# A decoder layer on one core: the front's planning constants, and the last tile's output in four pieces

## The chip, the cores and the metric

The kernel runs on one core of a Trainium2 chip. The metric is the device time of one execution in microseconds (us), as a median over runs. The core's engines are TensorE (PE in the profile, with its weight loads as PEld), VectorE (DVE), ScalarE (ACT), GpSimd (POOL) and SyncE (SP), which here only issues transfers. Each engine works through its own list of instructions in order, and engines wait for each other through semaphores.

## The reference

One post-norm decoder layer on x of 512 tokens by 1024 columns, all in float32:

```python
h = x @ w_in                                   # q, k, v, u, z: 512 columns each
attn = moba_attention(rope(q), rope(k), v)     # 8 heads of 64, block-sparse, causal
sg = gelu(u) * (W_s @ layer_norm(gelu(z)) + b) # gMLP gating in chunks of 128 tokens
mix = concat(rms_norm(attn), rms_norm(sg)) @ w_out
x = layer_norm(alpha * x + mix)
ffn = (silu(x @ w_gate) * (x @ w_up)) @ w_down # hidden width 2816
out = layer_norm(alpha * x + ffn)
```

## The kernel before

**Products.** Every float32 product is made of three matmuls of split operands: high times high, high times low, low times high. `mm3` issues such a triple (lines 252 to 254 of the profile). `split` makes the two halves: the high half is a copy on ACT (line 239) or, where `near` is set, on DVE (line 237); the low half is a subtraction on DVE or POOL (line 240). `split_dram` makes the low half in another way: ACT writes the negated high half (line 247), and a transfer issued by POOL adds the weights from DRAM onto it (line 248).

**Order.** The program is written as operations with a cost, a rank and dependences, given to `Order.op`. `Order.plan` runs a list schedule over five engines with these costs: the engine that is free first takes, of the operations that are ready, the one of lowest rank, and the result is the order in which the instructions are put on their engines. A cost thus changes no work; it changes the planned moment at which things are ready, and by that the order. `MM` is the planned cost of a triple of 512 columns. `RANK` gives the rank of each kind of work, and `TABLE` the cost of an ACT table change.

**Stages.** The front (about 0 to 225 us) has the v projection, then the parts of `SEQ`: q and k projections with rotary (`q0` to `q3`), attention of two heads each (`a0` to `a3`), the z and u projections, and `s` (`spatial`, `gmlp_norm`). `UNITS` is the order of the four query tiles in a head; a unit is scores, maximum, exponent, normalisation (line 464), transposes (line 471) through one PSUM bank, and the split of the transposed probabilities. `gmlp_norm` goes through four token tiles: a square on ACT (line 584), the power -0.5 on POOL (line 282), a scaling on DVE (line 586), four transposes (line 591), and a split. Then `out_half(4)` multiplies the gated half by the lower half of w_out, and `out_half(0)` the attention half by the upper half, whose operand `at_split` makes (lines 663 and 665). Projections and out-projections have rank `fill`: PE does them when nothing else is ready.

**First norm.** `layer_norm` runs tile by tile after `out_half(0)`: `add`, statistics (line 693), their sum (694), `rsqrt_col` (lines 281 and 282), then the normalised halves. With how = "A" or "P", ACT scales (line 706), DVE multiplies by the gain (708), and the bias is added at line 717: on DVE with "A", on POOL with "P". With "D" DVE does both steps in two fused operations per half (lines 702 and 713). Then each half is transposed (766) and split.

**FFN.** From there to about 440 us eleven `Pair`s of gate and up blocks are multiplied by a scheme with fewer block products (line 850). The first four pairs (`EARLY`) have their first blocks split ahead, in the front. `EARLY_LO` gives for each of their eight blocks how the low half is made: "M" is `split_dram`, "D" is `split` with DVE. Then the down projection runs to 557 us, and `finish` normalises and stores each tile: add (line 1012), `layer_norm` as `LN2` says ("ADAD"), and one store of 128 x 512 per half on SP (line 1017).

Groups of weights are named: `W(..., group="o1")` is w_out's second row tile. A group in `WHI` has its high half on DVE, one in `WPOOL` its low half on POOL. The groups that are passed are q0 to q3, z, u and o0 to o7; blocks of gate and up go through `whole`, which asks `EARLY_LO` and neither list.

Of the kernel before, what the change touches and what calls it, by code (L numbers as in the profile page):

```python
# [9 lines left out]
ALU = mybir.AluOpType  # L10
AX = mybir.AxisListType.X

P = 128
# [3 lines left out]
NT = S // P  # L17
# [12 lines left out]

SAME, CROSS, DMA_LAT, MM, MM256 = 0.15, 0.19, 1.9, 0.681, 0.36
GROW, GROW_LAT = 0.9, 10
SEQ = ('q1', 'a1', 'q0', 'z', 'q2', 'a0', 'u', 'q3', 's', 'a2', 'a3')
RANK = {"w": 5.0, "rope": 10.0, "att": 4.0, "gelu": -8.0, "z": -2.0, "s": -13.5, "fill": 15.0, "sq": -6.0, "ln": -10.5, "ffn": 8.0, "evac": 3.0}


UNITS = (2, 0, 3, 1)
NORM = "AADA"  # L40
LN1, LN2, LNT = "APAA", "ADAD", 0.3
WHI = ('o0', 'o2', 'q1')
WPOOL = ('e0', 'e1', 'e3', 'o1', 'o2', 'o4', 'z')
ROPE, ZSUB, ZMUL, ZG, ZB = "P", "P", "P", "P", "P"


class Buf:
# [139 lines left out]
def build(tc, cp, wp, ap, ps, xt, xtok, w_vqk, w_zu, w_out, w_gu, w_dn, wsp, cst, rows, cols, out):  # L187
    nc = tc.nc
    od = Order()
    V, A, PL, PE = nc.vector, nc.scalar, nc.gpsimd, nc.tensor  # L190
# [5 lines left out]
    def dve(n, fn, r, w, per=1.042, **k):  # L196
        od.op("DVE", 0.066 + 0.001 * per * n, fn, r, w, **k)
# [4 lines left out]
    def dma(kb, fn, r, w, **k):  # L202
        od.op("SP", max(0.46, kb / 352.0), fn, r, w, **k)

    def pe(n, fn, r, w, **k):
        od.op("PE", n, fn, r, w, **k)

    def const(shape, tag=None, dtype=F32):
        return od.buf(cp, shape, dtype, tag)

    def work(shape, tag, bufs=1, dtype=F32):
        return od.buf(ap, shape, dtype, tag, bufs)
# [4 lines left out]
    def prob(dtype=F32):  # L217
        return work([P, S], "pr", 4, dtype)

    def small(n):  # L220
        return work([P, n], "sm", 24)

    def bank(tag, bufs):
        return od.buf(ps, [P, S], F32, tag, bufs)

    def pj():
        return bank("pj", 4)
# [22 lines left out]
    def mm3(cost, o, lh, ll, rh, rl, start, stop, r, w, **k):  # L250
        def fn():
            PE.matmul(o(), lhsT=lh(), rhs=rh(), start=start, stop=False)  # L252
            PE.matmul(o(), lhsT=lh(), rhs=rl(), start=False, stop=False)  # L253
            PE.matmul(o(), lhsT=ll(), rhs=rh(), start=False, stop=stop)  # L254

        pe(cost, fn, r, w, **k)

    class W:


        def __init__(self, src, tag=None, mid=None, group=None):
# [10 lines left out]
            every = slice(0, WCH)  # L272
            dma(512, lambda: nc.sync.dma_start(raw.t, src), [], [raw], base=RANK["w"])
            if mid is not None:
                mid(raw)
            split(WCH, lambda: raw.t, lambda: self.hi(every), lambda: self.lo(every), [raw], hk, lk, group in WPOOL,
                  near=group in WHI, base=RANK["w"])

# [10 lines left out]
    mhalf, ones = const([P, 32]), const([P, 2])  # L289
# [3 lines left out]
    def row(i):  # L293
        b = work([P, D], "kl", 2)
        dma(512, lambda: nc.sync.dma_start(b.t, bass.AP(tensor=rows.tensor, offset=rows.offset + 3 * S + i * D,
                                                        ap=[[0, P], [1, D]])), [], [b], base=RANK["rope"])
        return b
# [16 lines left out]
    def v_step(c, kk, raw, wh, wl):  # L314
        k = 2 * c + kk
        cs = slice(kk * 512, kk * 512 + 512)
        xr = prob()
        dma(256, lambda: nc.sync.dma_start(raw.t[:, cs], w_vqk[c][:, cs]), [], [(raw, kk)], base=RANK["w"])
        split(512, lambda: raw.t[:, cs], lambda: wh.t[:, cs], lambda: wl.t[:, cs],
              [(raw, kk)], [(wh, kk)], [(wl, kk)], base=RANK["w"])  # L320
        pieces = ((0, 1), (1, NT)) if k == 0 else ((0, NT),)
        for t0, t1 in pieces:
            def piece(t0=t0, t1=t1, ts=slice(t0 * P, t1 * P)):
                sub = [(k, t) for t in range(t0, t1)]
                dma(64 * (t1 - t0), lambda: nc.sync.dma_start(xr.t[:, ts], xt[k][:, ts]), [], [(xr, t0)], base=RANK["w"])
                split((t1 - t0) * P, lambda: xr.t[:, ts], lambda: xh.t[:, k, ts], lambda: xl.t[:, k, ts], [(xr, t0)],
# [295 lines left out]
    xk = work([P, NT, D], "xl")  # L622
# [3 lines left out]
    def out_half(c0, spare, left, done, wide=None):  # L626
        ws = [W(w_out[c0 + k], spare if k == 3 else None, group=f"o{c0 + k}") for k in range(4)]
        for t in range(NT):
            ts = slice(t * P, t * P + P)
            b = [bank("sc", 2), bank("sc", 2)] if t == wide else [pj(), pj()]  # L630
            for k in range(4):
                for hf in range(2):
                    def one(k=k, hf=hf, t=t, ts=ts, b=b, hs=slice(hf * 512, hf * 512 + 512)):
                        lh, ll, keys = left(k, t, ts)
                        mm3(MM, lambda: b[hf].t, lh, ll, lambda: ws[k].hi(hs), lambda: ws[k].lo(hs), k == 0, k == 3,
                            [*keys, *ws[k].key], [b[hf]])

                    one()
            done(t, b)
# [42 lines left out]

    HV = [slice(0, 512), slice(512, 1024)]

    def layer_norm(t, add, done, how):

        keys = [(xk, (t, 0)), (xk, (t, 1))]
        y = lambda i: xk.t[:, t, HV[i]]
        st, mv, rs, nmr = small(12), small(2), small(1), small(1)
        g, b = LN  # L690
        for i in range(2):
            add(i, keys[i])
            dve(512, lambda i=i: V.bn_stats(out=st.t[:, 6 * i:6 * i + 6], in_=y(i)), [keys[i]], [(st, i)])
        dve(12, lambda: V.bn_aggr(out=mv.t, in_=st.t.rearrange("p (a b) -> p a b", b=6)), [st], [mv])
        rsqrt_col(rs, lambda: mv.t[:, 1:2], [mv], 1, 1.0, LN_EPS)
        if how != "D":
            dve(1, lambda: V.scalar_tensor_tensor(out=nmr.t, in0=mv.t[:, 0:1], scalar=-1.0, in1=rs.t, op0=ALU.mult,
                                                  op1=ALU.mult), [mv, rs], [nmr])
        for i in range(2):
            k, gi, bi = [keys[i]], lambda i=i: g.t[:, HV[i]], lambda i=i: b.t[:, HV[i]]  # L700
            if how == "D":
                dve(560, lambda i=i, gi=gi: V.scalar_tensor_tensor(
                    out=y(i), in0=y(i), scalar=mv.t[:, 0:1], in1=gi(), op0=ALU.subtract, op1=ALU.mult), [mv, g, *k], k,
                    lock=True)
            else:
                act(512, lambda i=i: A.activation(y(i), y(i), AF.Identity, bias=nmr.t, scale=rs.t), [rs, nmr, *k], k,
                    aps=2)
                dve(512, lambda i=i, gi=gi: V.tensor_tensor(out=y(i), in0=y(i), in1=gi(), op=ALU.mult), [g, *k], k,
                    lock=True)
        for i in range(2):  # L710
            k, bi = [keys[i]], lambda i=i: b.t[:, HV[i]]
            if how == "D":
                dve(560, lambda i=i, bi=bi: V.scalar_tensor_tensor(
                    out=y(i), in0=y(i), scalar=rs.t, in1=bi(), op0=ALU.mult, op1=ALU.add), [rs, b, *k], k,
                    lock=True)
            else:
                either("P" if how == "P" else "D", 512, lambda E, i=i, bi=bi: E.tensor_tensor(
                    out=y(i), in0=y(i), in1=bi(), op=ALU.add), [b, *k], k)
            done(i, k)
# [197 lines left out]
            self.gated(c, self.h1, self.i1, 0, -1.0)  # L917

    pairs = [Pair(p) for p in range(NP)]
    EARLY, EARLY_LO = 4, "MMMMMMMM"  # L920
    EARLY_SLOTS = (("wr", "wr"), (0, 1), ("wr", "wr"), (0, 1))
    for p in range(EARLY):
        blks = [whole(Raw(p, 3 * i, EARLY_SLOTS[p][i]), 2 * p + i) for i in range(2)]
# [47 lines left out]
    yb = [[pj(), pj()], [pj(), pj()], [bank("sc", 2), bank("sc", 2)], [bank("tp", 1), bank("pv", 1)]]  # L971

    last = work([P, KT, S], "xh", 1, F32R)
# [16 lines left out]
    def down_mm(f, t, hf, w):  # L990
        w, (hh, hl), keys = w
        ts = slice(t * P, t * P + P)
        hs = slice(hf * 512, hf * 512 + 512)
        mm3(MM, lambda: yb[t][hf].t, lambda: hh()[:, ts], lambda: hl()[:, ts],
            lambda: w.hi(hs), lambda: w.lo(hs), f == 0, f == FT - 1, [*w.key, *keys], [yb[t][hf]])

    TAIL = 6
    for f in range(FT - TAIL):
        w = down_w(f)
# [6 lines left out]
    def finish(t):  # L1006
        for i in range(2):
            for f in wt:
                down_mm(f, t, i, wt[f])

        def add(i, key):
            dve(512, lambda: V.scalar_tensor_tensor(out=xk.t[:, t, HV[i]], in0=xk.t[:, t, HV[i]], scalar=ALPHA,
                                                    in1=yb[t][i].t, op0=ALU.mult, op1=ALU.add),
                [yb[t][i], key], [key])

        def done(i, key):
            dma(256, lambda: nc.sync.dma_start(out[t * P:t * P + P, HV[i]], xk.t[:, t, HV[i]]), key, [])

        od.base = RANK["ffn"] - 0.1 * (t + 1)
        layer_norm(t, add, done, LN2[t])  # L1020
        od.base = RANK["ffn"]

    for t in range(NT):
        finish(t)
# [65 lines left out]
```

## Time and profile before

| | us |
|---|---|
| median of 3 runs | 566.88 (566.67 to 567.62) |
| the profiled execution | 566.79 |
| its span in the trace | 565.0 |
| PE busy in the span | 545.7 |

The profiled execution is 1.79 us longer than its span, which is what lies around the traced instructions, and 0.09 us under the median. A busy PE is not a PE at its peak: the ends of matmuls are modelled. The granted clock of TensorE is a share of full speed: 1.00 is 2.4 GHz and 0.50 is 1.2 GHz. Idle time of PE is 565.0 - 545.7 = 19.3 us, and some of it is before the first and after the last matmul.

### The profile page before, as it was taken

How to read it: one execution, taken by the hardware profiler on the slowest of the kernel's cores; microseconds unless marked ns; L12 is line 12 of the kernel's file. 1: busy time of each engine (PE TensorE's matmuls, PEld its weight loads, DVE VectorE, ACT ScalarE, POOL GpSimd, SP SyncE). 2: the span in 40 equal slices, each digit the busy share in tenths (PEclk: the TensorE clock that was granted, in tenths of full speed). 3: DMA queues.
4: the chain of work that ended last, by engine and by line, in shares of the span. 5: the costliest groups of instructions: out<-in, count | busy, mean ns of one | idle time of the engine just before them, and what ended most of it. 6: DMA issues, size and time to landing. Idle time of an engine off the chain costs nothing.

```text
span 565.0 us, 8788 instructions
## 1 busy us (share of the span) xinstructions
PE 545.7 (97%) x3360; PEld 488.1 (86%) x3360; DVE 406.6 (72%) x701; ACT 290.0 (51%) x492; POOL 158.2 (28%) x120
## 2 busy tenths in 40 slices
PE   9999999999699999999999999999999999999994
PEld 6887888888488878999999999999999888888883
DVE  5645868889885879979998788878877623324485
ACT  6324787687774768745444544554455432323211
POOL 0016229823311531234452342333322200000011
PEclk9999999999699999999999999999999999999998
DMA  8746412144811898635432333233124333232311
GB/s 261 261 133 160 129 59 93 57 143 134 307 43 45 244 280 205 171 109 187 131 131 89 137 98 106 97 113 113 37 75 150 117 107 105 82 113 79 108 74 74
DMA packets 23241, 72.85 MB, mean 129 GB/s; under 512 B 3104, under 2 KB 3616, under 8 KB 23200
## 3 DMA queue, kind: packets, MB, share of 16 engines
q1 hardware_dynamic: 22048, 68.11, 37.2%
q0 software_dynamic: 1152, 4.19, 4.0%
q8 instruction: 26, 0.43, 0.3%
q14 instruction: 15, 0.12, 0.1%
HBM read 66.00 MB, written 2.10 MB: 121 GB/s over the span
## 4 chain that ended last, share of the span: by engine, by line
PE 84%; DMA 5%; ACT 5%; DVE 3%; issue 2%; SPq 1%; POOL 0%; DVEq 0%; POOLq 0%; ACTq 0%
PE pj L850 19%; PE sc L850 16%; PE pj L252 11%; PE pj L253 11%; PE pj L254 11%; DMA wr<-w_gu 2%; PE sc L252 2%; PE sc L253 2%; PE sc L254 2%; PE pv L488 2%; PE tp L471 1%; DMA wr<-w_out 1%; DMA zg<-w_gu 1%; DMA qk<-qk 1%; PE pv L252 1%
## 5 line engine op out<-in xcount | busy, mean ns | idle before, releaser
L240 DVE TENSOR_TENSOR wl<-wr,wh 128x1024 fp32r<-128x1024 f32 (+1 forms) x56 | 71.7, 1284 | 63.0 <-ACT wh L239 62.9
L239 ACT ACTIVATE wh<-wr 128x1024 fp32r<-128x1024 f32 (+1 forms) x59 | 58.9, 999 | 82.4 <-PE sc L254 54.0
L850 PE MATMUL pj<-qk,wh 128*128 128x256 f32 x352 | 64.4, 283 | 0.0
L850 PE MATMUL sc<-xh,wh 128*128 128x256 f32 x352 | 64.3, 283 | 0.0
L850 PEld LDWEIGHTS pj<-qk,wh 128*128 128x128 f32 x352 | 55.0, 192 | 0.0
L850 PEld LDWEIGHTS sc<-xh,wh 128*128 128x128 f32 x352 | 54.9, 192 | 0.0
L282 POOL TENSOR_TENSOR sm<-sm,only 128x1 f32<-128x1 f32 (+2 forms) x17 | 18.7, 1099 | 124.8 <-DVE sm L281 124.8
L850 PE MATMUL pj<-V,wh 128*128 128x256 f32 x288 | 52.6, 283 | 0.0
L850 PE MATMUL pj<-qk,wl 128*128 128x256 f32 x176 | 50.0, 284 | 0.1
L850 PE MATMUL sc<-xh,wl 128*128 128x256 f32 x176 | 49.9, 283 | 0.0
L252 PE MATMUL pj<-wh,xh 128*128 128x512 f32 x114 | 47.0, 412 | 0.0
L253 PE MATMUL pj<-wl,xh 128*128 128x512 f32 x114 | 45.0, 395 | 0.0
L850 PEld LDWEIGHTS pj<-V,wh 128*128 128x128 f32 x288 | 45.0, 192 | 0.0
L850 PE MATMUL pj<-V,wl 128*128 128x256 f32 x144 | 40.8, 283 | 0.0
L254 PE MATMUL pj<-wh,xl 128*128 128x512 f32 x96 | 37.9, 395 | 0.0
L240 POOL TENSOR_TENSOR wl<-wr,wh 128x1024 fp32r<-128x1024 f32 x7 | 17.7, 2523 | 69.5 <-ACT wh L239 66.6
L239 ACT ACTIVATE wh<-tp 128x512 fp32r<-128x512 f32 x33 | 19.6, 595 | 30.1 <-PE sc L850 20.4
L850 PEld LDWEIGHTS pj<-qk,wl 128*128 128x128 f32 x176 | 33.8, 192 | 0.3 <-DVE wl L240 0.3
L850 PEld LDWEIGHTS sc<-xh,wl 128*128 128x128 f32 x176 | 33.8, 192 | 0.0
L850 PE MATMUL sc<-ug,wh 128*128 128x256 f32 x176 | 32.2, 284 | 0.9 <-ACT wh L239 0.9
L850 PEld LDWEIGHTS sc<-ug,wh 128*128 128x128 f32 x176 | 27.5, 192 | 1.2 <-ACT wh L239 1.1
L253 PE MATMUL pj<-wl,pr 128*128 128x512 f32 x72 | 28.0, 390 | 0.0
(338 smaller groups left out, 1510.6 us busy)
## 6 DMA issues: line engine op xcount, KB each, us to landing
wr<-w_dn SPq DMA_DIRECT2D x22, 512.0 KB, 3.3
wr<-w_gu SPq DMA_DIRECT2D x20, 512.0 KB, 3.4
zg<-w_gu SPq DMA_DIRECT2D x18, 512.0 KB, 3.4
kl<-w_gu SPq DMA_DIRECT2D x14, 512.0 KB, 3.3
wr<-w_vqk SPq DMA_DIRECT2D x8, 512.0 KB, 3.6
wr<-w_zu SPq DMA_DIRECT2D x8, 512.0 KB, 3.5
wr<-w_out SPq DMA_DIRECT2D x8, 512.0 KB, 4.2
wr<-w_vqk SPq DMA_DIRECT2D x8, 256.0 KB, 4.5
```

The lines of the kernel that those rows point to most:

```text
L239: act(n, lambda: A.activation(hi(), src(), AF.Copy), rs, ws_hi, **k)
L240: either("P" if far else "D", n, lambda E: E.tensor_tensor(out=lo(), in0=src(), in1=hi().bitcast(F32), op=ALU.subtract), [*rs, *ws_hi], ws_lo,
L252: PE.matmul(o(), lhsT=lh(), rhs=rh(), start=start, stop=False)
L253: PE.matmul(o(), lhsT=lh(), rhs=rl(), start=False, stop=False)
L254: PE.matmul(o(), lhsT=ll(), rhs=rh(), start=False, stop=stop)
L282: od.op("POOL", 0.3 + 0.165 * n, lambda: PL.tensor_tensor(out=o.t, in0=v.t, in1=mhalf.t[:, :n], op=ALU.pow), [v, mhalf], [o], lock=True)
L471: PE.transpose(tp.t[:, j * P:j * P + P], p.t[:, j * P:j * P + P], ident.t)
L488: PE.matmul(pv.t[:, j * P:], lhsT=vs.t[:, j, h, :], rhs=pt.t[:, j * S:j * S + w], start=j == 0 and i == 0, stop=j == NT - 1 and i == 1)
L850: PE.matmul(o, lhsT=lh(w), rhs=buf.t[:, s + rh, x], start=first and side == k == i == 0, stop=k == 3 and i == 2, skip_group_check=True)
```

## The change

The planned cost of a triple is 0.643 instead of 0.681 in the v, q, k, z and u projections; the out and down projections keep 0.681 under the name `MMD`. Three ranks and the step between the first norm's tiles have other numbers. The first norm's bias goes to POOL for tiles 0 and 2 instead of tile 1. The high halves of o1 and o3 are made on DVE. Of the eight early blocks, the first and the last have their low half made by DVE. The last tile's bias step is made in four pieces of 256 columns, each stored at once, by ACT's and SP's queues in turn; and a power operation on constants, whose result nobody reads, is put on POOL ahead of the last tile's own.

```diff
--- before.py
+++ after.py
@@ -30,18 +30,20 @@
 
 
 
-SAME, CROSS, DMA_LAT, MM, MM256 = 0.15, 0.19, 1.9, 0.681, 0.36
+SAME, CROSS, DMA_LAT, MM, MMD, MM256 = 0.15, 0.19, 1.9, 0.643, 0.681, 0.36
 GROW, GROW_LAT = 0.9, 10
 SEQ = ('q1', 'a1', 'q0', 'z', 'q2', 'a0', 'u', 'q3', 's', 'a2', 'a3')
-RANK = {"w": 5.0, "rope": 10.0, "att": 4.0, "gelu": -8.0, "z": -2.0, "s": -13.5, "fill": 15.0, "sq": -6.0, "ln": -10.5, "ffn": 8.0, "evac": 3.0}
+RANK = {"w": 5.0, "rope": 10.0, "att": 4.0, "gelu": -8.0, "z": -2.0, "s": -13.5, "fill": 15.0, "sq": -6.0, "ln": -5.8, "ffn": 10.8, "evac": 4.6}
 
 
 UNITS = (2, 0, 3, 1)
 NORM = "AADA"
-LN1, LN2, LNT = "APAA", "ADAD", 0.3
-WHI = ('o0', 'o2', 'q1')
-WPOOL = ('e0', 'e1', 'e3', 'o1', 'o2', 'o4', 'z')
+LN1, LN2, LNT = "PAPA", "ADAD", 0.05
+WHI = ('o0', 'o1', 'o2', 'o3', 'q1')
+WPOOL = ('o1', 'o2', 'o4', 'z')
 ROPE, ZSUB, ZMUL, ZG, ZB = "P", "P", "P", "P", "P"
+
+EARLY, EARLY_LO = 4, "DMMMMMMD"
 
 
 class Buf:
@@ -632,7 +634,7 @@
                 for hf in range(2):
                     def one(k=k, hf=hf, t=t, ts=ts, b=b, hs=slice(hf * 512, hf * 512 + 512)):
                         lh, ll, keys = left(k, t, ts)
-                        mm3(MM, lambda: b[hf].t, lh, ll, lambda: ws[k].hi(hs), lambda: ws[k].lo(hs), k == 0, k == 3,
+                        mm3(MMD, lambda: b[hf].t, lh, ll, lambda: ws[k].hi(hs), lambda: ws[k].lo(hs), k == 0, k == 3,
                             [*keys, *ws[k].key], [b[hf]])
 
                     one()
@@ -682,7 +684,7 @@
 
     HV = [slice(0, 512), slice(512, 1024)]
 
-    def layer_norm(t, add, done, how):
+    def layer_norm(t, add, done, how, last=None):
 
         keys = [(xk, (t, 0)), (xk, (t, 1))]
         y = lambda i: xk.t[:, t, HV[i]]
@@ -690,6 +692,10 @@
         g, b = LN
         for i in range(2):
             add(i, keys[i])
+            if last and i == 1:
+                v = small(1)
+                od.op("POOL", 0.5, lambda: PL.tensor_tensor(out=v.t, in0=ones.t[:, 0:1], in1=mhalf.t[:, 0:1], op=ALU.pow),
+                      [ones, mhalf, keys[1]], [v], lock=True)
             dve(512, lambda i=i: V.bn_stats(out=st.t[:, 6 * i:6 * i + 6], in_=y(i)), [keys[i]], [(st, i)])
         dve(12, lambda: V.bn_aggr(out=mv.t, in_=st.t.rearrange("p (a b) -> p a b", b=6)), [st], [mv])
         rsqrt_col(rs, lambda: mv.t[:, 1:2], [mv], 1, 1.0, LN_EPS)
@@ -709,6 +715,14 @@
                     lock=True)
         for i in range(2):
             k, bi = [keys[i]], lambda i=i: b.t[:, HV[i]]
+            if last:
+                for j in range(2):
+                    c = slice(512 * i + 256 * j, 512 * i + 256 * j + 256)
+                    dve(280, lambda c=c: V.scalar_tensor_tensor(
+                        out=xk.t[:, t, c], in0=xk.t[:, t, c], scalar=rs.t, in1=b.t[:, c], op0=ALU.mult, op1=ALU.add),
+                        [rs, b, *k], [(xk, (t, i, j))], lock=True)
+                    last(j, c, (xk, (t, i, j)))
+                continue
             if how == "D":
                 dve(560, lambda i=i, bi=bi: V.scalar_tensor_tensor(
                     out=y(i), in0=y(i), scalar=rs.t, in1=bi(), op0=ALU.mult, op1=ALU.add), [rs, b, *k], k,
@@ -917,7 +931,6 @@
             self.gated(c, self.h1, self.i1, 0, -1.0)
 
     pairs = [Pair(p) for p in range(NP)]
-    EARLY, EARLY_LO = 4, "MMMMMMMM"
     EARLY_SLOTS = (("wr", "wr"), (0, 1), ("wr", "wr"), (0, 1))
     for p in range(EARLY):
         blks = [whole(Raw(p, 3 * i, EARLY_SLOTS[p][i]), 2 * p + i) for i in range(2)]
@@ -991,7 +1004,7 @@
         w, (hh, hl), keys = w
         ts = slice(t * P, t * P + P)
         hs = slice(hf * 512, hf * 512 + 512)
-        mm3(MM, lambda: yb[t][hf].t, lambda: hh()[:, ts], lambda: hl()[:, ts],
+        mm3(MMD, lambda: yb[t][hf].t, lambda: hh()[:, ts], lambda: hl()[:, ts],
             lambda: w.hi(hs), lambda: w.lo(hs), f == 0, f == FT - 1, [*w.key, *keys], [yb[t][hf]])
 
     TAIL = 6
@@ -1017,7 +1030,13 @@
             dma(256, lambda: nc.sync.dma_start(out[t * P:t * P + P, HV[i]], xk.t[:, t, HV[i]]), key, [])
 
         od.base = RANK["ffn"] - 0.1 * (t + 1)
-        layer_norm(t, add, done, LN2[t])
+        def piece(j, c, key):
+            if j:
+                dma(128, lambda: nc.sync.dma_start(out[t * P:t * P + P, c], xk.t[:, t, c]), [key], [])
+            else:
+                od.op("ACT", 0.1, lambda: A.dma_start(out[t * P:t * P + P, c], xk.t[:, t, c]), [key], [])
+
+        layer_norm(t, add, done, LN2[t], piece if t == NT - 1 else None)
         od.base = RANK["ffn"]
 
     for t in range(NT):
```

## Rows read from the trace of the kernel before

**Rows 1.** The page's list of busy time (share of the span) and instructions.

```profile
PE 545.7 (97%) x3360; PEld 488.1 (86%) x3360; DVE 406.6 (72%) x701; ACT 290.0 (51%) x492; POOL 158.2 (28%) x120
```

**Rows 2.** Windows of 5 us: busy PE, PEld, DVE, ACT, POOL, clock, DMA share, GB/s.

```profile
140.00:145.00 5.00, 1.60 (x11) 1.17 (x9) 4.54 (x10) 4.49 (x10) 2.28 (x2) 0.85 0.76 207
145.00:150.00 5.00, 3.00 (x11) 2.36 (x11) 3.78 (x7) 4.48 (x9) 2.37 (x2) 0.50 0.98 366
150.00:155.00 5.00, 5.00 (x20) 3.88 (x19) 3.98 (x11) 2.26 (x5) 1.38 (x2) 0.62 0.90 309
```

**Rows 3.** What PE waited for: us in total, times, longest.

```profile
PE pj L591 <- DVE ug L586: 2.7, 1, 2.7
PE tp L471 <- DVE sm L281: 2.0, 1, 2.0
...
PE sc L432 <- DMA qk<-qk: 1.1, 1, 1.1
```

**Rows 4.** Timeline around PE's longest stall (start us, us, engine, line, operation).

```profile
139.97 1.32 ACT L663 ACTIVATE xh<-atr,only 128x512 fp32r<-128x512 f32 x2
...
143.22 0.73 DVE L665 SCALAR_TENSOR_TENSOR xh<-atr,only,xh 128x512 fp32r<-128x512 f32 x1
144.41 1.23 DVE L240 TENSOR_TENSOR wl<-wr,wh 128x1024 fp32r<-128x1024 f32 x1 [0.46 <-ACT wh L239]
145.56 0.74 DVE L586 SCALAR_TENSOR_TENSOR ug<-ug,sm,only 128x512 f32<-128x512 f32 x1
```

**Rows 5.** The chain that ended last, after the stall and near the end (start, us, what).

```profile
150.19 0.43 PE pj L254
...
548.98 0.23 PE tp L252
```

**Rows 6.** One window of 20 us in the first norm, columns as in rows 2.

```profile
205.00:225.00 20.00, 17.37 (x128) 15.77 (x127) 15.82 (x31) 16.83 (x25) 4.99 (x6) 1.00 0.95 227
```

**Rows 7.** Timeline in the first norm: POOL's bias addition, and PE's waits.

```profile
206.05 1.30 POOL L717 TENSOR_TENSOR xl<-xl,kl 128x512 f32<-128x512 f32 x1 [1.69 <-DVE xl L708]
...
209.51 0.39 PE L850 MATMUL pj<-V,pth 128*128 128x256 f32 x1 [0.92 <-ACT V L239]
...
215.07 0.63 PE L766 MATMUL tp<-only,xl 128*128 128x128 f32 x4 [0.74 <-issue]
```

**Rows 8.** Single lines of code: duration of one, ns, min/median/max, first and last start.

```profile
L247 ACT ACTIVATE wl<-wr x2: 1044/1045/1046, 207.4 to 213.5; 128x1024 fp32r<-128x1024 f32 x2
L237 DVE TENSOR_SCALAR wh<-wr x4: 686/694/695, 23.1 to 185.5; 128x1024 fp32r<-128x1024 f32 x4
L717 DVE TENSOR_TENSOR xl<-xl,kl x10: 643/684/687, 199.7 to 555.6; 128x512 f32<-128x512 f32 x10
L240 DVE TENSOR_TENSOR wl<-kl,wh x12: 1207/1225/2817, 258.5 to 427.1; 128x1024 fp32r<-128x1024 f32 x12
L566 DVE SCALAR_TENSOR_TENSOR ug<-pj,only,ug x8: 476/480/486, 127.6 to 134.0; 128x256 f32<-128x256 f32 x8
```

**Rows 9.** Timeline of the last tile's norm on DVE.

```profile
557.17 0.69 DVE L1012 SCALAR_TENSOR_TENSOR xl<-xl,pv 128x512 f32<-128x512 f32 x1 [0.92 <-PE pv L254]
...
558.94 1.40 DVE L702 SCALAR_TENSOR_TENSOR xl<-xl,sm,kl 128x512 f32<-128x512 f32 x2
560.26 1.41 DVE L713 SCALAR_TENSOR_TENSOR xl<-xl,sm,kl 128x512 f32<-128x512 f32 x2
```

**Rows 10.** POOL's powers in the second norm, first and last of four.

```profile
538.75 0.56 POOL L282 TENSOR_TENSOR sm<-sm,only 128x1 f32<-128x1 f32 x1 [96.85 <-DVE sm L281]
...
559.10 0.99 POOL L282 TENSOR_TENSOR sm<-sm,only 128x1 f32<-128x1 f32 x1 [7.61 <-DVE sm L281]
```

**Rows 11.** The last store's issue on SP, and issues to landing (KB each, median us).

```profile
561.69 0.33 SPq L1017 DMA_DIRECT2D out<-xl  x1
...
rt<-rt SPq DMA_DIRECT2D x32, 64.0 KB, 2.0
...
out<-xl SPq DMA_DIRECT2D x8, 256.0 KB, 2.1
```

## The prediction

> **What bounds the kernel now.** I read the page's busy times first: PE is busy 545.7 of 565.0 us [rows 1], so the kernel is bound by TensorE, and 19.3 us are all that any order can win. The change adds and removes no matmul. The questions are where those 19.3 us lie, and which of them an order of issue can reach.
>
> The last tile's addition starts on DVE at 557.17, after a wait for the last matmul [rows 9], so 565.0 - 557.1 = 7.9 us are the tail. Next I went through the span in windows. Only one stretch has PE clearly idle: between 140 and 150 us PE is busy 1.60 and 3.00 us of 5 [rows 2], which leaves 3.4 + 2.0 = 5.4 us. The list of PE's waits names the same place: 2.7 us for line 586 and 2.0 us before a transpose, while the front before it has one wait of 1.1 us for a transfer [rows 3]. That the fill work was used up there is seen in the same windows: ACT is busy 4.49 and 4.48 us and DVE 4.54 and 3.78 us while PE is not. So for these 10 us the heads of ACT's and DVE's lists set the pace.
>
> The stall costs more than its idle time. The clock granted there falls to 0.50 and is at 0.62 in the next window [rows 2], and in the chain a matmul of 512 columns takes 0.43 us at 150.19 where it takes 0.23 us near the end [rows 5]. That is the lower of its two levels. It costs 5 x (1 - 0.62) = 1.9 us in the third window and some 0.4 us at the end of the second, where PE has come back to its matmuls: an estimate of 2.3 us. **The stall is worth 5.4 + 2.3 = 7.7 us.**
>
> The third place is the first norm: between 205 and 225 us PE is busy 17.37 of 20 us [rows 6], 2.6 us idle.
>
> **The front, edit by edit.** Some numbers change no order. The norm's rank goes from -10.5 to -5.8, but what stands between these two values (the GELUs, the last square) is an input of the norm. The ranks of the FFN and of its evacuations pass those of rotary and attention, which are over by then. The names e0, e1 and e3 are asked for nowhere. These I cost at nothing; if one of them does meet a competitor, it adds to the spread below.
>
> *The planned triple.* The chip needs 3 x 0.23 = 0.69 us [rows 5], so 0.681 was nearly true and 0.643 is too low. It holds for 160 triples (32 for v, 64 for q and k, 64 for z and u), so the plan sees PE 160 x 0.038 = 6.1 us earlier at the end of the projections than it will be. The order of ACT's and DVE's lists in the stall is dealt anew. What can that give? At the stall stand things that nobody needs for 40 us: two operand splits for the attention half on ACT, 1.32 us, and two on DVE, of which one is shown with 0.73 us; a weight split of 1.23 us stands directly ahead of line 586, which PE awaits [rows 4]. Behind it on DVE wait line 586 and then the split that frees the one PSUM bank of the transposes. Moving these away could shorten the stall by 1.32 on ACT and by about 1.5 + 1.2 on DVE. Upper bound: the whole stall, -7.7 us. Lower bound: fill work is used earlier by the whole 6.1 us, and the stall is that much longer, +6.1 us. No row shows the new order. I take half of the stall, **-3.8 us**: the 1.3 to 2.7 us of postponable work stand in it, and what the idle time loses the clock gives back besides (2.3 of 5.4 us).
>
> *High halves of o1 and o3.* Two copies leave ACT (about 1.05 us each, as the row for a pass of that size shows) and come to DVE at 0.69 us each [rows 8]. PE has the lower out-projection to do meanwhile; without that cover it would be 1.4 us.
>
> *Early blocks.* Each of the two that change saves ACT a pass of 1.04 us, POOL one issue and the transfer system one of eight accumulating transfers, and costs DVE a subtraction of 1.23 us [rows 4, 8]. DVE gets +2.5 us.
>
> *Bias of the first norm.* Tile 1's two additions go from POOL, 1.30 us each [rows 7], to DVE, 0.68 us [rows 8]. PE's wait of 0.92 us at 209.51 hangs on tile 1's last half, so some 0.6 us come back. Tile 2's go the other way, and its transposes already waited 0.74 us at 215.07 [rows 7]: 0.6 us are lost again. DVE has two additions fewer, 2 x 0.68 = -1.4 us.
>
> DVE thus gets 1.4 + 2.5 - 1.4 = +2.5 us in a stage where it is busy 15.82 of 20 us, and ACT 16.83 [rows 6]; ACT loses 2 x 1.04 + 2 x 1.05 = 4.2 us, and ACT is what PE waited for at 209.51 [rows 7]. I take **0** for this stage, between -2.6 (all waits gone) and +2.5 (DVE's growth all on the path).
>
> **The tail.** The last norm's four fused operations follow each other on DVE without a gap: two start 560.26 - 558.94 = 1.32 us after the other two, so one each 0.66 us, and the last at 560.92 [rows 9]. The power ends at 559.10 + 0.99 = 560.09 [rows 10], and the third operation starts at 560.26 because the second has just left. So the power is covered, and making it shorter gives nothing. Nor would the idle power shorten it: after 96.85 us of idleness a power took 0.56 us, and after 7.61 us it took 0.99 us [rows 10], so it isn't idleness that makes it slow. The idle power reads constants alone, runs when POOL is free, and is covered by the second bias step.
>
> By the Trainium skill, page "SBUF — State Buffer", section "Who interferes with whom", a DVE instruction with two SBUF inputs and a GpSimd instruction that reads SBUF exclude each other. The trace agrees: the powers of 0.99 us are those beside line 702.
>
> Two operations of 512 columns become four of 256. A fused operation of 256 took 0.48 us [rows 8] where one of 512 takes 0.74: 0.26 less, so the spacing falls from 0.66 to 0.40 us. The last piece is ready at 560.26 + 3 x 0.40 + 0.48 = 561.94 instead of 560.92 + 0.74 = 561.66, **+0.28 us**. Its transfer has 128 KB instead of 256. The old one took 2.1 us from issue to landing, and one of 64 KB took 2.0 [rows 11]; by these it saves at most 0.1, and if time went by size it would save 1.05. The row of 64 KB is the nearer in kind (fixed time above all), but two stores that follow at 0.66 us share the same transfer engines, so I take **-0.2 us**. The second queue gives nothing: SP needs 0.33 us for an issue [rows 11], less than the 0.40 us between pieces. What a store from ACT costs no row shows: nothing, or an issue like SP's of 0.33 us, with 0.40 us of slack before the last piece. Tail: **+0.1 us**, between -0.8 and +0.6.
>
> By the Trainium skill, page "Trainium Kernel Development and Optimization", section "Key Constraints", transfers from several queues run on the same 16 engines and only issue time is saved; by that rule too the tail gains nothing from ACT's queue.
>
> **Sum.** 566.79 (the profiled execution) - 3.8 + 0 + 0.1 = 563.1 us. The median of the runs is 0.09 us above that execution, which I leave out.
>
> **The rivals.**
> 1. *The stall closes and the norm's waits with it*: 566.8 - 7.7 - 2.6 = 556.5 us. For it: ACT is relieved in both places. Against it: DVE was as full as ACT in the stall.
> 2. *Nothing moves*: the tail is even, and the stall is only shifted by the new order. ACT and DVE have the same work to do before PE can go on: 566.9 us.
> 3. *The fill runs out sooner*: more triples are planned between the steps of attention, PE loses nothing by that before 140 us, but q3's projection ends earlier against `gmlp_norm`, and PE waits for the same ACT and DVE heads. Up to +6.1, so 572.9 us; half of it, 569.8. It decides once the fill ends more than 1.1 us earlier than what the heads give back.
> 4. *DVE becomes the bound in the first norm*: +2.5 us as above, 569.3 us. POOL's additions make it worse where they block DVE: a split beside POOL took 2.817 instead of 1.225 us [rows 8]. The section named above says as much of operations with two SBUF inputs. It decides when DVE's list falls behind by more than ACT's relief.
>
> **How the numbers follow.** The forecast gets 0.46, with a range of its own from 559.3 to 565.6. Rival 1 gets 0.12, rival 2 0.16, rival 3 0.16, rival 4 0.10. A measurement of this kernel can tell 0.2%, 1.1 us. Faster: 0.46 + 0.12 = 0.58. Same: 0.16. Slower: 0.26. For 8 in 10, the range leaves out most of rival 1 and the upper part of rivals 3 and 4, about 0.1 at each end: 558.5 to 570.5.
>
> **What would show it.** Right: the windows around 140 to 155 us have PE busy for at least 2 us more and a granted clock above 0.62; the first norm keeps about 2.6 us of PE idleness; from the last matmul to the end there are 7.9 us, and the last power still takes 0.99 us beside line 702. Wrong: PE's idle time before 190 us grows, a new wait for DVE appears between 195 and 250 us, or the tail changes by more than 0.5 us.

## The result and the profile after

The median went from 567.07 us (four runs of before) to 559.79 us: a ratio of 0.9878, with a 95% interval of 0.9855 to 0.9902. The profiled execution took 559.55 us, 7.2 us less than the 566.79 of before. PE's busy time, from the page:

```profile
PE 543.3 (97%) x3360; PEld 485.4 (87%) x3360; DVE 411.3 (74%) x705; ACT 285.9 (51%) x488; POOL 157.0 (28%) x121
```

Windows of the stall and of the first norm in the kernel after (columns as in [rows 2]):

```profile
140.00:145.00 5.00, 3.61 (x19) 2.25 (x18) 4.97 (x11) 4.95 (x10) 1.22 (x2) 1.00 0.76 220
145.00:150.00 5.00, 3.69 (x19) 2.92 (x20) 4.56 (x7) 4.94 (x10) 1.66 (x2) 1.00 0.89 339
```
```profile
205.00:225.00 20.00, 20.00 (x170) 20.00 (x170) 18.92 (x34) 17.80 (x29) 5.98 (x6) 1.00 0.69 184
```

PE's idle time in the stall is 1.39 + 1.31 = 2.7 us instead of 5.4 [rows 2], and the clock stays at 1.00 where it fell to 0.50. In the first norm's window PE has no idle time at all, where 2.6 us were lost [rows 6]. But 0.6 of these is a wait for an evacuation (line 872, 886 after) that has only moved out of the window; before, then after:

```profile
224.14 0.51 PE L850 MATMUL pj<-V,ptl 128*128 128x256 f32 x2 [0.61 <-ACT cs L872]
226.39 0.50 PE L864 MATMUL pj<-V,wh 128*128 128x256 f32 x2 [0.69 <-ACT cs L886]
```

So the norm's own gain is 2.0 us. What PE still waits for:

```profile
PE pj L255 <- DVE sm L283: 1.3, 1, 1.3
...
PE pj L254 <- ACT znh L241: 1.0, 1, 1.0
PE sc L864 <- ACT wh L241: 1.0, 1, 1.0
```

The waits of 2.7 and 2.0 us [rows 3] have become one of 1.3 and one of 1.0. The third line lies behind the norm (at 242.16).

The account closes. Up to the last tile's addition (549.58 us after, 557.17 before) PE was idle 549.58 - 543.3 = 6.3 us instead of 557.17 - 545.7 = 11.5: -5.2 us: 2.7 in the stall, 2.0 in the norm, and 0.5 before 100 us, where the wait for a transfer [rows 3] has shrunk from 1.1 to 0.3 us and one of 0.3 is new. PE's busy time is 2.4 us shorter for the same 3360 matmuls, which is the clock: the stall and the 4 us behind it [rows 2] were the only stretch in which PE had work at the lower clock. The tail of this execution is 0.4 us longer. Together -7.2 us.

The tail on DVE and on POOL, and the stores by ACT's and SP's queues (KB each, median us to landing):

```profile
549.58 0.69 DVE L1025 SCALAR_TENSOR_TENSOR xl<-xl,pv 128x512 f32<-128x512 f32 x1 [0.92 <-PE pv L256]
...
551.35 1.41 DVE L708 SCALAR_TENSOR_TENSOR xl<-xl,sm,kl 128x512 f32<-128x512 f32 x2
552.67 1.67 DVE L721 SCALAR_TENSOR_TENSOR xl<-xl,sm,kl 128x256 f32<-128x256 f32 x4
```
```profile
543.35 0.55 POOL L284 TENSOR_TENSOR sm<-sm,only 128x1 f32<-128x1 f32 x1 [5.67 <-DVE sm L283]
543.87 0.55 POOL L697 TENSOR_TENSOR sm<-only,only 128x1 f32<-128x1 f32 x1
551.51 0.99 POOL L284 TENSOR_TENSOR sm<-sm,only 128x1 f32<-128x1 f32 x1 [7.09 <-DVE sm L283]
```
```profile
out<-xl ACTq DMA_DIRECT2D x2, 128.0 KB, 1.8
out<-xl SPq DMA_DIRECT2D x2, 128.0 KB, 1.8
```

The idle power (line 697) runs at 543.87, straight after the third tile's, 7.1 us ahead of the one it stands in front of, and that one takes 0.99 us as before [rows 10]. The four pieces last 1.67 us on DVE instead of 1.41 [rows 9], 0.26 more. The median store lands 1.8 us after its issue instead of 2.1 [rows 11]; the last one alone took 1.89 instead of 2.04, 0.15 less. So the last store lands 6.67 us after the start of the last tile's addition instead of 6.56, 0.1 later. The other 0.3 of the 0.4 us lie behind that landing.

### The profile page after: what moved, and what is told of

It is laid out like the page before. It is cut to its first block, busy times and chain, and to the rows that moved or that the text cites. A ratio compares the mean times of both kernels' runs of the same rounds, so it can differ in the third digit from the quotient of the medians.

```text
span 557.8 us, 8795 instructions
## 1 busy us (share of the span) xinstructions
PE 543.3 (97%) x3360; PEld 485.4 (87%) x3360; DVE 411.3 (74%) x705; ACT 285.9 (51%) x488; POOL 157.0 (28%) x121
## 4 chain that ended last, share of the span: by engine, by line
PE 93%; DVE 2%; ACT 2%; DMA 2%; issue 0%; DVEq 0%
PE pj L864 22%; PE sc L864 16%; PE pj L254 12%; PE pj L255 12%; PE pj L256 12%; PE sc L256 2%; PE sc L255 2%; PE sc L254 2%; PE pv L490 2%; PE tp L473 2%; DMA qk<-qk 1%; PE sc L435 1%; PE sc L434 1%; PE pv L256 1%; PE tp L256 1%; PE tp L255 1%
## 5 line engine op out<-in xcount | busy, mean ns | idle before, releaser
L242 DVE TENSOR_TENSOR wl<-wr,wh 128x1024 fp32r<-128x1024 f32 (+1 forms) x56 | 69.9, 1249 | 61.7 <-ACT wh L241 61.4
L284 POOL TENSOR_TENSOR sm<-sm,only 128x1 f32<-128x1 f32 (+2 forms) x17 | 16.8, 991 | 141.5 <-DVE sm L283 138.8
L242 DVE TENSOR_TENSOR wl<-tp,wh 128x512 fp32r<-128x512 f32 x33 | 22.6, 684 | 8.3 <-ACT wh L241 8.0
```

What stands on the lines that cost most here:

```text
L242: either("P" if far else "D", n, lambda E: E.tensor_tensor(out=lo(), in0=src(), in1=hi().bitcast(F32), op=ALU.subtract), [*rs, *ws_hi], ws_lo,
L284: od.op("POOL", 0.3 + 0.165 * n, lambda: PL.tensor_tensor(out=o.t, in0=v.t, in1=mhalf.t[:, :n], op=ALU.pow), [v, mhalf], [o], lock=True)
```

## The experiments

The runs of one kernel scatter by about 0.5% (before: 564.1 to 570.8 us over all comparisons), so the verdicts below lean on the windows and waits as much as on the medians. One control needs no run: with the ranks, the step between the norm's tiles and the names e0, e1, e3 changed alone, every engine's list of instructions is the same as before, row by row.

**1. The planned cost alone.**

```diff
-SAME, CROSS, DMA_LAT, MM, MM256 = 0.15, 0.19, 1.9, 0.681, 0.36
+SAME, CROSS, DMA_LAT, MM, MMD, MM256 = 0.15, 0.19, 1.9, 0.643, 0.681, 0.36
...
-    mm3(MM, ...)    # out_half and down_mm
+    mm3(MMD, ...)
```

> Kernel before with the planned triple at 0.643 in the v, q, k, z and u projections, nothing else. If the planned cost deals the order of the stall anew by itself: PE idle between 140 and 150 us falls from 5.4 to about 2.7 us, the clock stays at 1.00, and the time falls by about 5 us, to 562; the first norm keeps its 2.6 us of idle PE. Rival, that the stall was shortened by the edits to the out-projection weights and the early blocks: the stall stays within 1 us of 7.7 and the time is 566 to 568. Rival, that the fill runs out sooner: slower, 568 to 573.

Measured: 566.65 us (10 runs, 563.47 to 569.39), ratio 0.9992 (0.9965 to 1.0019): no difference that can be measured. Its windows:

```profile
140.00:145.00 5.00, 3.17 (x12) 1.72 (x12) 4.52 (x8) 4.95 (x12) 1.89 (x2) 1.00 0.79 270
145.00:150.00 5.00, 4.22 (x23) 3.55 (x24) 4.97 (x10) 4.89 (x10) 0.55 (x1) 1.00 0.87 277
...
200.00:225.00 25.00, 23.55 (x187) 22.62 (x186) 21.78 (x41) 21.77 (x35) 5.49 (x7) 1.00 0.89 221
225.00:250.00 25.00, 23.29 (x190) 22.70 (x189) 21.46 (x34) 12.78 (x23) 8.00 (x5) 1.00 0.50 148
250.00:300.00 50.00, 48.00 (x397) 47.45 (x396) 45.97 (x58) 23.61 (x40) 21.41 (x16) 1.00 0.37 123
```

The first theory was half right. The cost alone makes the stall short (1.83 + 0.78 = 2.6 us idle, full clock), but PE then idles 1.5, 1.7 and 2.0 us in the norm and behind it. Its profiled execution, 563.87, is 2.9 us below that of before; the median keeps only 0.4 of that.

**2. Everything but the cost.**

```diff
-SAME, CROSS, DMA_LAT, MM, MMD, MM256 = 0.15, 0.19, 1.9, 0.643, 0.681, 0.36
+SAME, CROSS, DMA_LAT, MM, MMD, MM256 = 0.15, 0.19, 1.9, 0.681, 0.681, 0.36
```

> Kernel after with the planned triple back at 0.681. If the planned cost made the stall shorter: the stall of about 7.7 us is back, only the first norm's 2.6 us are won, 564 to 565. If the edits to weights, blocks and bias did it: as after, about 560. If the edits only pay together with the cost: slower than 565.

Measured: 573.55 us, ratio 1.0119 (1.0076 to 1.0161): slower than before. The old stall is back, and the norm has a worse one. PE, then ACT's list:

```profile
PE tp L780 <- POOL xl L731: 3.8, 1, 3.8
PE pj L593 <- DVE ug L588: 2.5, 1, 2.5
```
```profile
199.93 1.06 ACT L248 ACTIVATE pth<-wr 128x1024 fp32r<-128x1024 f32 x1 [6.96 <-DMA wr<-w_gu]
200.90 1.04 ACT L249 ACTIVATE znh<-wr 128x1024 fp32r<-128x1024 f32 x1
203.91 3.16 ACT L712 ACTIVATE xl<-xl,sm,sm 128x512 f32<-128x512 f32 x4 [1.97 <-DVE sm L703]
```

The list of waits names POOL's bias, but ACT's list shows more: the copy of an early block (line 248) stands at the head for 6.96 us, until its weights land. The norm's scaling (line 712), from which the bias follows, stands behind it, but waits for DVE 1.97 us longer. POOL's list says why:

```profile
202.24 0.86 POOL L250 DMA_DIRECT2D znh<-w_gu  x1 [9.30 <-ACT znh L249]
202.80 0.88 POOL L284 TENSOR_TENSOR sm<-sm,only 128x1 f32<-128x1 f32 x1
```

The norm's power (line 284), which DVE and then the scaling need, stands behind the issue of an accumulating transfer (line 250), and that waits 9.30 us for the second pass over the same late block. DVE had the power's input ready at 197.3.

**3. The front without the new tail (an edit of after), and 4. the tail without the front** (an edit of before, which takes over `piece` and the new `layer_norm` and leaves all constants).

```diff
-        layer_norm(t, add, done, LN2[t], piece if t == NT - 1 else None)     # 3
+        layer_norm(t, add, done, LN2[t], None)
...
-        layer_norm(t, add, done, LN2[t])                                     # 4
+        layer_norm(t, add, done, LN2[t], piece if t == NT - 1 else None)
```

> Kernel after with the tail of before (two stores of 128 x 512 on SP, no idle power). The tail after is 8.2 us from the last matmul to the end against 7.9 before. If the pieces or the second queue cost this: 559.4, 0.3 to 0.4 below after, with the tail at 7.9. If the difference is the spread of single executions: 559.8 as after. If the pieces won something: 560.1 or more.

> Kernel before with the new tail alone. If the tail costs: 567.3 to 567.5, with 8.2 us from the last matmul to the end. If it does nothing: 567.0. If it wins: 566.7 or less. The last power takes 0.99 us in all three; if the idle power warms POOL, it takes 0.55 us.

Measured: the front alone 561.52 us, ratio 0.9905 (0.987 to 0.994), which overlaps with that of after; the tail alone 566.58, ratio 0.9984 (0.9961 to 1.0007). From the start of the last tile's addition to the end of the span, the four traces with the old tail (before, runs 1, 3 and 12) show 7.8 to 8.1 us, the ten with the new one 7.7 to 8.3. Up to the landing of the last store they are steady: 6.55 to 6.57 us with the old tail, 6.60 to 6.68 with the new one. So the new tail costs 0.1 us, too little for the medians to tell; what scatters lies behind the last landing.

**5 to 7. One edit of the front taken back from after.**

```diff
-LN1, LN2, LNT = "PAPA", "ADAD", 0.05        # 5
+LN1, LN2, LNT = "APAA", "ADAD", 0.05
...
-EARLY, EARLY_LO = 4, "DMMMMMMD"             # 6
+EARLY, EARLY_LO = 4, "MMMMMMMM"
...
-WHI = ('o0', 'o1', 'o2', 'o3', 'q1')        # 7
+WHI = ('o0', 'o2', 'q1')
```

> Kernel after with the first norm's bias as before (POOL for tile 1, DVE for the others). With the planned triple at 0.681 the bias on POOL cost PE a wait of 3.8 us. If the bias on POOL is bad in itself: faster than after by 1 to 2 us, 558 to 559. If it is the edit that freed the first norm at the new cost: PE waits of 1 to 1.5 us are back between 200 and 225 us, 561. If it is neutral there: 560.

> Kernel after with all eight early blocks through the accumulating transfers. If these blocks carry what the cost alone did not give (ACT passes and transfers): PE's waits between 180 and 300 us go from 1.7 back to 4 or 6 us, 563 to 565. If they are a side matter: 560.

> Kernel after with the high halves of o1 and o3 back on ACT. ACT gets 2.1 us, DVE loses 1.4 us. If ACT is what the first norm waits for: 1 to 2 us of PE waits between 180 and 225 us, 561 to 562. If not: 560 or, by DVE's relief, 559.

Measured: bias 561.24 us, ratio 0.9918 (0.9894 to 0.9943), whose interval overlaps with that of after; early blocks 562.29, ratio 0.993 (0.9908 to 0.9953), slower than after; the two copies 567.55, ratio 1.0009 (0.9984 to 1.0034): two copies of some 1 us each on the other engine take the whole gain away. The same stretch in after and in runs 5, 6 and 7:

```profile
200.00:225.00 25.00, 24.96 (x200) 24.06 (x199) 23.44 (x43) 22.80 (x37) 6.87 (x7) 1.00 0.70 185
200.00:225.00 25.00, 24.11 (x189) 23.13 (x188) 22.45 (x43) 22.47 (x36) 4.97 (x7) 1.00 0.77 192
200.00:225.00 25.00, 22.52 (x161) 21.36 (x160) 20.52 (x39) 21.18 (x33) 6.67 (x7) 0.93 0.88 213
200.00:225.00 25.00, 21.42 (x138) 19.46 (x139) 20.02 (x32) 18.38 (x29) 8.88 (x8) 0.86 0.78 194
```

PE idles 0.0 us there in after, and 0.9, 2.5 and 3.6 us in the three. In run 7, windows, then ACT's list, then PE's waits:

```profile
205.00:210.00 5.00, 2.01 (x9) 1.38 (x9) 4.07 (x7) 5.00 (x9) 1.62 (x2) 0.82 0.76 171
210.00:215.00 5.00, 4.86 (x22) 4.56 (x23) 4.21 (x11) 2.57 (x4) 1.69 (x4) 0.50 1.04 243
```
```profile
202.89 1.06 ACT L248 ACTIVATE wh<-wr 128x1024 fp32r<-128x1024 f32 x1 [2.87 <-DMA wr<-w_gu]
...
204.80 0.58 ACT L784 ACTIVATE pr<-tp 128x512 f32<-128x512 f32 x1
```
```profile
200.05 0.66 PE L780 MATMUL tp<-only,xl 128*128 128x128 f32 x4 [0.54 <-POOL xl L731]
206.65 0.66 PE L780 MATMUL tp<-only,xl 128*128 128x128 f32 x4 [2.04 <-DVE V L242]
```

The transposes of 200.05 are done at 200.71, and their evacuation (line 784) begins at 204.80: ACT stood 2.87 us at an early copy whose weights hadn't landed. PE's next transposes wait for that PSUM bank, and the clock falls to 0.50 after it. The same is in the trace of before, and I hadn't read it there. POOL, PE and then ACT:

```profile
203.06 1.29 POOL L717 TENSOR_TENSOR xl<-xl,kl 128x512 f32<-128x512 f32 x1 [3.49 <-DVE xl L708]
...
205.47 0.60 PE L766 MATMUL tp<-only,xl 128*128 128x128 f32 x4
...
206.48 1.06 ACT L246 ACTIVATE wh<-wr 128x1024 fp32r<-128x1024 f32 x1 [1.91 <-DMA wr<-w_gu]
207.45 1.04 ACT L247 ACTIVATE wl<-wr 128x1024 fp32r<-128x1024 f32 x1
208.40 0.57 ACT L770 ACTIVATE pr<-tp 128x512 f32<-128x512 f32 x1
208.87 0.59 ACT L239 ACTIVATE V<-tp 128x512 fp32r<-128x512 f32 x1
```

The first half of tile 1 has its bias at 204.35 and its transposes at 206.07; the evacuation begins at 208.40, and the split behind it (line 239) is what PE awaits at 209.51 [rows 7]. In after, the copy's wait is 0.30 us. Run 6 is not of this kind: PE waits 1.92 us for such a split, but no early copy on ACT waits more than 0.40 us behind 195 us; one of 1.63 us stands earlier, at 190.88. Its cause wasn't followed.

**8. A cost between the two**, in the kernel after.

```diff
-SAME, CROSS, DMA_LAT, MM, MMD, MM256 = 0.15, 0.19, 1.9, 0.643, 0.681, 0.36
+SAME, CROSS, DMA_LAT, MM, MMD, MM256 = 0.15, 0.19, 1.9, 0.662, 0.681, 0.36
```

> Kernel after with the planned triple at 0.662, half way between the two. If the time follows the cost (a trend: a triple that is planned shorter lets attention come later): between 560 and 573.5, near 566. If each value is a deal of its own: anywhere from 560 to 575, and which waits come back can't be told ahead.

Measured: 576.8 us, ratio 1.0188 (1.0168 to 1.0208). So 0.681, 0.662 and 0.643 give 573.55, 576.8 and 559.79 us: no trend. PE's longest wait and ACT's list:

```profile
PE tp L676 <- DVE sqa L508: 4.6, 1, 4.6
```
```profile
193.72 1.06 ACT L248 ACTIVATE pth<-wr 128x1024 fp32r<-128x1024 f32 x1 [4.14 <-DMA wr<-w_gu]
194.68 0.61 ACT L506 ACTIVATE rt<-atr 128x512 f32<-128x512 f32 x1
```

Once more an early copy waits for its weights, this time ahead of attention's last square (line 506), on which PE's sums wait.

**9. The copies on ACT, in the order of after.** The operation is planned as DVE's, so that all lists stay as they are but for these two copies.

```diff
+            def copy():
+                if near in ('o1', 'o3'):
+                    A.activation(hi(), src(), AF.Copy)
+                else:
+                    V.tensor_scalar(hi(), src(), 1.0, None, op0=ALU.mult)
...
-            dve(n, lambda: V.tensor_scalar(hi(), src(), 1.0, None, op0=ALU.mult), rs, ws_hi, per=0.52, lock=True, **k)
+            dve(n, copy, rs, ws_hi, per=0.52, lock=True, **k)
```

> Kernel after in its own order on every engine, with only the two copies of o1 and o3 done by ACT instead of DVE at the same place of the program. With the list dealt anew for these copies on ACT, the kernel took 567.55. If the copies' own time on ACT costs that: 566 to 568. If it is the order that the plan makes of them, in which ACT's early-block copies stand ahead of the evacuations that PE waits for: 560 to 561, and PE's waits between 180 and 225 us stay under 1 us.

Measured: 560.99 us, ratio 0.9914 (0.9885 to 0.9944), as after within its interval, and 6.6 us below run 7. PE idles 1.35 us between 200 and 225 us, a little over what was expected:

```profile
200.00:225.00 25.00, 23.65 (x183) 22.30 (x182) 22.43 (x41) 22.67 (x36) 6.88 (x7) 1.00 0.79 207
```

So the copies' time on ACT is at most 1.2 of the 7.8 us between run 7 and after; the rest is the order that the plan makes when they count as ACT's.

**10. Run 7 without the accumulating transfers**, in its own order. The kernel leaves out what these transfers add to the low halves.

```diff
-        od.op("POOL", GROW, lambda: nc.gpsimd.dma_start(lo(), dram, accum_op=ALU.add), ws_lo, ws_lo, lat=GROW_LAT, **k)
+        od.op("POOL", GROW, lambda: None, ws_lo, ws_lo, lat=GROW_LAT, **k)
```

> The kernel with the copies of o1 and o3 back on ACT (567.55), in its own order, with the six accumulating transfers left out (the low halves of these six blocks lack the weights, so this part of the product is left out of the result). There ACT waits 2.87 us for early weights at 202.89, with the evacuation that PE awaits behind it. If the accumulating transfers make these weights late: that wait falls under 1 us, PE's idle time between 180 and 225 us falls from 4.1 to about 1 us, the clock there stays at 1.00, and the time is 561 to 563. If the order of the additions and splits makes it: 566 to 568.

Measured: 561.58 us, ratio 0.9923 (0.9895 to 0.9952), 6.0 us below run 7. ACT no longer waits there; the window:

```profile
200.00:225.00 25.00, 23.49 (x185) 22.28 (x184) 24.26 (x42) 20.82 (x35) 4.86 (x5) 1.00 0.30 106
```

PE idles 1.5 us there instead of 3.6, and the DMA share is 0.30 instead of 0.78. The load that the copy at 202.89 waited for, from its issue to landing in run 7 and in run 10:

```profile
wr<-w_gu SPq DMA_DIRECT2D x1, 512.0 KB, 12.3
wr<-w_gu SPq DMA_DIRECT2D x1, 512.0 KB, 4.6
```

Its issue is as early in both (190.55 and 189.53), so the transfers were what made these weights late.

**11 and 12. A plan that knows of the late landing**, for after and for before.

```diff
             dma(512, lambda: nc.sync.dma_start(self.t(), self.src), [], [self.key], base=PREP)
+            if late:                        # 6.0 for the early blocks
+                od.ops[-1].lat = late
```

> Kernel after, with the plan told that the early blocks' weights land 6.0 us after their issue instead of 1.9 (the transfers themselves are the same). If late landings ahead of evacuations are what the plan gets wrong, its copies move behind the evacuations and nothing is lost: 559 to 561. If each order is a deal of its own: anywhere between 558 and 575.

> Kernel before, with the plan told that the early blocks' weights land 6.0 us after their issue. Up to 180 us nothing changes, so the stall of 7.7 us stays. If ACT's waits for early weights (1.91 us at 206.48, with the evacuation of the transposes behind it) make the first norm's 2.6 us: these fall under 1 us, 564.5 to 566. If POOL's bias addition makes them, as the prediction said: 566.5 to 567.5, with PE's wait at the first early product still there.

Measured: 561.23 us, ratio 0.9916 (0.9887 to 0.9945), and 566.46 us, ratio 0.9981 (0.995 to 1.0011). In run 11 no early copy on ACT waits for its weights behind 195 us, and PE still idles 2.7 us between 200 and 225 us, most of it waiting for the evacuation of line 888 (886 in after). In run 12 ACT's wait at 206.48 is gone, but PE's wait at an early product is only handed on, to DVE's split of the same tile:

```profile
PE pj L852 <- DVE V L240: 1.1, 1, 1.1
```

PE idles 1.6 us there, not under 1, the clock falls to 0.66 between 210 and 215 us, where before has 1.00, and the median doesn't move: inconclusive for before. No run beat after.

## Why the prediction was right

The forecast was 563.1 us and the measured time is 559.79: inside the range, and inside the likeliest case's own, near its lower end. The total was right; of its steps, the working of the norm and the work that moves in the stall were not.

**The stall (-3.8, between -7.7 and +6.1).** The size came to -2.7 us of idle time and -2.4 us of clock, -5.1 in all. The place was right, and that the cost deals the order anew: run 1 shows that the cost by itself shortens the stall, run 2 that without it the stall is back. What the order moves isn't what I had named. ACT and PE in before, then in after:

```profile
142.32 0.62 ACT L584 ACTIVATE rt<-ug 128x512 f32<-128x512 f32 x1
...
148.96 0.80 PE L252 MATMUL pj<-wh,znh 128*128 128x512 f32 x1 [0.64 <-ACT znh L239]
```
```profile
136.67 0.62 ACT L586 ACTIVATE rt<-ug 128x512 f32<-128x512 f32 x1
139.90 1.33 ACT L665 ACTIVATE xh<-atr,only 128x512 fp32r<-128x512 f32 x2
...
142.37 0.50 PE L254 MATMUL pj<-wh,znh 128*128 128x512 f32 x1 [0.99 <-ACT znh L241]
```

The attention half's splits, the work that I wanted postponed, still stand in the stall (139.90, as at 139.97 in before [rows 4]). What moved is the first token tile's square, with which `gmlp_norm` begins: it was behind these splits and is now ahead of them, so the gated half's first product starts at 142.37 instead of 148.96, and PE has work. The nine kernels at 0.643 and the one at 0.662 all have the square ahead (135.2 to 137.6 us), the four at 0.681 behind (142.3 to 143.8).

The clock's part was taken as halved with the stall; it went wholly, since the shorter stall here didn't bring the clock down. That is partly luck: in run 3 it did (last section).

**The first norm (0, between -2.6 and +2.5).** This step was mis-sized, and its working was wrong; that it came out inside its bounds is luck. It came to -2.6 in the window, the lower bound, and to -2.0 without the wait that only moved. I had put PE's wait at 209.51 [rows 7] down to POOL's bias additions, by way of tile 1's last half, and added up moved work. But it hangs on the first half, which POOL had left at 204.35. Taking the bias back (run 5) brings 0.9 us of PE's idle time back. What holds PE at 209.51 in before (1.3 of the 2.0 us), in runs 2 and 7, and before the norm in run 8, begins at a head of ACT's list: an early block's copy waiting 1.91 to 6.96 us for weights, ahead of work that PE needs. Run 10 shows that the accumulating transfers make these weights late; run 9 shows that the order decides whether that hurts. It may not be the only cause: in runs 6 and 11 PE idles 2.5 and 2.7 us with no such wait behind 195 us.

**Edits added up one by one.** That the terms can be summed was the unspoken step that failed. The cost alone gives no measurable gain and the rest alone costs 1.2%, yet together they give -1.2%. Two copies that I took for covered decide 7 us, through the order.

**The tail (+0.1).** Right, and in its parts: 0.26 us later on DVE where I had 0.28, 0.15 us earlier to land where I took 0.2. The tail as a whole is no test of it, since it scatters by 0.5 us behind the last landing. The idle power warms nothing: the powers took 0.55 us where DVE ran nothing beside them and 0.99 us beside line 708. By the Trainium skill, page "SBUF — State Buffer", section "Who interferes with whom", the two exclude each other where DVE has two SBUF inputs; these rows agree again.

**The rivals.** The first came true for the norm but not for the whole stall. That the fill would run out sooner wasn't seen in any kernel with the cost at 0.643: PE's idle time between 140 and 150 us was 2.6 to 3.1 us in all nine of them. DVE did not become the bound, though it was busy 18.92 of 20 us in the norm.

Still open is why the plan at 0.643 and 0.662 has the square ahead of the splits. Its rank, that of `s`, is the lowest in `RANK`, so the plan takes it as soon as it counts it as ready; what else moves that moment wasn't tried.

## What to carry to other kernels

In a kernel whose order comes from a planner, read ahead of each PE stall the list of the engine that feeds it, and the list of the engine behind that one, and look for an instruction that waits for a transfer with urgent work behind it; the list of PE's waits names only the last link. Don't price the edits of such a kernel one by one: keep the order fixed and change the work, or keep the work and change the order, to see which of the two it is. A constant of the planner has no slope to follow: between two values that differ by 0.02 us there were 17 us.

## What the runs showed that wasn't expected

The same order with the same idle time can bring the clock down or not. The front alone (run 3) has the front of after:

```profile
140.00:145.00 5.00, 3.59 (x20) 2.20 (x19) 4.51 (x12) 4.95 (x12) 1.27 (x2) 1.00 0.85 262
145.00:150.00 5.00, 3.72 (x13) 2.79 (x12) 4.83 (x8) 4.66 (x10) 1.15 (x2) 0.71 0.90 293
```

Its order is that of after up to the tail. PE idles 1.41 + 1.28 us, as in after, but the clock granted in the second window is 0.71 instead of 1.00. PE is busy 544.8 us in that execution and 543.3 in that of after, so the clock was worth about 1.5 us. That is part of the scatter between runs of one kernel.
